# A two-layer diffusion transformer on one core: the FFN's down projection by seven products of quarters, with its sums in seven PSUM banks and the sums of quarters on GpSimd

## The chip, the core and the metric

The kernel runs on one core of a Trainium2 chip. A time is the device time of one execution in microseconds (us). TensorE (PE) does the matrix products, ScalarE (ACT) and VectorE (DVE) the elementwise work, GpSimd (POOL) some more of it, and SyncE (SP) issues most DMAs.

## The reference, cut to what matters

Two layers work on 256 context and 1024 latent tokens of width 1024. Each has a mixing part (windowed attention and a Fourier mix), which the change leaves alone, and then the feed-forward network:

```python
def swiglu(h, w_gate, w_up, w_down):
    return (jax.nn.silu(h @ w_gate) * (h @ w_up)) @ w_down
...
        hf = modulate(rmsnorm(x_mid, norm_pre_ffn[i]), sh2, sc2)
        x = x_mid + g2 * rmsnorm(swiglu(hf, w_gate[i], w_up[i], w_down[i]), norm_post_ffn[i])
```

The hidden width is 2816. The context tokens go through the same weights; in the second layer only the latent tokens go through the FFN.

## The kernel before

Features lie on partitions, tokens along the free dimension. The FFN works on two blocks of tokens: two of 640 in layer 0, two of 512 in layer 1. The hidden width is 22 tiles of 128, taken as `NP` = 11 pairs f. A product in f32 is made of three in f16: an operand is split into hi (a rounded copy, made on ACT) and lo (the rest, made on DVE by a SCALAR_TENSOR_TENSOR from the source and hi), and PE adds hi by hi, lo by hi and hi by lo in PSUM.

**Up and gate** (`ffn_up`) multiply two by two quarters by seven products instead of eight: a pair of weight tiles and a half of the width against two halves of a block. `sums` makes the weight's quarters and their four sums (L499 to L502, 128x512 each, on DVE) and the hi and lo parts (L487 and L488); it does so for the first `AHEAD` = 4 pairs in an earlier stage (tiles `wa`, kept in DRAM as `wc`), and in the last part of up and gate for the other seven (tiles `ww`, 14 of gate and up per layer). `product` inside `ffn_up` (PE, L1116) leaves sums in PSUM, from which DVE and ACT assemble a 2 by 2 of quarters C11 to C22; hi and lo of these (L1163, L1164) are the hidden operand. Eight of the first block's eleven pairs are kept in SBUF (`KEPT`), the others go to DRAM (`hs`) and are read again.

**Down** (`ffn_down`) takes one block in a pass: for each output tile m of eight and each group of `PAIRS` it loads the weights (512 or 384 KB), makes hi (L1253, ACT) and lo (L1254, DVE) pair by pair in 128x256, and PE (L1261) runs through both halves of the pair over the whole block. Two PSUM tiles take turns, and ACT moves a finished one out (L1267). Layer 0 has two passes. Layer 1 has three: its second block is done in two halves, so that the norm of the first half runs beside the products of the second.

`postnorm` is the norm after the FFN: `stats` and `spread` (PE transposes into a PSUM tile, ACT copies), `scale` (L741, DVE) and the addition of the residual read from DRAM (L813, on DVE, or every second one on POOL with `share`). `mod(i)` makes a third of the next layer's modulation vectors on DVE (L674).

Parts are written as Python generators that `mix` interleaves by given costs; the scheduler of the framework then fixes the order of each engine, and pools (four `raw` tiles, eight `w`, five `tmp`, two double PSUM tiles `sc` and four single ones `ps`) bound how far a part runs ahead.

## Time and profile before

| | |
|---|---|
| median of three runs | 2480.28 us (2477.31 to 2480.35) |
| profiled execution, its time | 2482.05 us |
| its span, mean granted PE clock | 2480.2 us, 0.984 |
| up and gate, layer 0 | 564.4 to 1106.6 us |
| down, layer 0 | 1108.6 to 1411 us |
| up and gate, layer 1 | 1806.5 to about 2229 us |
| down, layer 1 | 2231 to 2463 us |
| from the last product to the end | 17.2 us |

Busy times are sums over the instructions of an engine, and a stage is a stretch between the first and the last product of its line. In a row of groups stand line, engine, operation, what is written and read, shapes and count, then busy time and mean ns, then the idle time of the engine just before them with what ended it. In a row of a timeline stand start and length in us.

### The profile page before, as it was taken

The page shows a single profiled execution, that of the slowest core. Times are in us where ns is not written, and L with a number is a line of the kernel's source. Part 1 is how long each engine was busy: PE and PEld are TensorE (multiplying, and loading weights), DVE is VectorE, ACT ScalarE, POOL GpSimd, SP SyncE. Part 2 cuts the span into 40 slices and gives each one's busy share as a digit, 9 for nine tenths or more (in the row PEclk, how much of TensorE's full clock was granted, in tenths as well). Part 3 has the DMA queues.
Part 4 walks back from the last instruction along what each step waited for, and adds up shares of the span by engine and source line. Part 5 has one row for each costly group of instructions (what it writes and reads, how often), then busy time and mean ns, then how long its engine had stood idle before and what let it go on. Part 6 is the DMA issues. An engine that isn't in the chain of part 4 may idle for free. (4 is left out here: it accounts for less than half of the span.)

```text
span 2480.2 us, 44040 instructions
## 1 busy us (share of the span) xinstructions
PE 2353.2 (95%) x17212; PEld 1867.4 (75%) x17212; DVE 1695.2 (68%) x3434; ACT 1347.7 (54%) x2587; POOL 190.5 (8%) x200
## 2 busy tenths in 40 slices
...
GB/s 308 177 134 188 129 146 132 146 260 254 198 187 145 113 130 162 145 183 361 285 254 154 87 127 50 35 18 52 203 340 208 159 60 86 77 117 240 132 251 128
DMA packets 157377, 406.83 MB, mean 164 GB/s; under 512 B 17488, under 2 KB 34288, under 8 KB 157168
## 3 DMA queue, kind: packets, MB, share of 16 engines
...
q14 instruction: 74, 0.61, 0.1%
...
## 5 line engine op out<-in xcount | busy, mean ns | idle before, releaser
L1116 PE MATMUL p<-ffn,ww 128*128 128x320 f16 (+1 forms) x7392 | 926.8, 288 | 34.2 <-ACT ww L487 7.8
L1116 PEld LDWEIGHTS <-ww 128*128 128x128 f16 x7392 | 724.0, 98 | 233.3 <-issue 27.7
L1261 PEld LDWEIGHTS <-wd 128*128 128x128 f16 x3696 | 362.2, 98 | 166.3 <-ACT wd L1253 9.1
L1261 PE MATMUL acc<-hid,wd 128*128 128x320 f16 (+2 forms) x2544 | 334.4, 293 | 6.1 <-ACT wd L1253 5.8
L1254 DVE SCALAR_TENSOR_TENSOR wd<-raw,dn,wd 128x256 f16<-128x256 f32 x440 | 187.4, 480 | 132.8 <-ACT wd L1253 126.7
L543 PE MATMUL accn<-arena,hi 128*128 128x320 f32 (+1 forms) x992 | 260.9, 332 | 1.7 <-DVE PTX L234 0.7
L1253 ACT ACTIVATE wd<-raw,dn 128x256 f16<-128x256 f32 x440 | 187.2, 496 | 130.7 <-PE acc L1261 81.5
L543 PE MATMUL acc<-arena,hi 128*128 128x320 f32 (+2 forms) x928 | 209.5, 331 | 4.9 <-ACT X L1070 3.1
L1261 PE MATMUL acc<-X,wd 128*128 128x320 f16 (+1 forms) x1152 | 191.9, 328 | 2.7 <-ACT wd L1253 2.4
L543 PEld LDWEIGHTS accn<-arena,hi 128*128 128x128 f32 x992 | 174.1, 190 | 18.4 <-issue 7.5
L543 PEld LDWEIGHTS acc<-arena,hi 128*128 128x128 f32 x928 | 155.1, 191 | 23.6 <-issue 6.6
L543 PE MATMUL accn<-arena,lo 128*128 128x320 f32 (+1 forms) x496 | 159.3, 324 | 0.0
L703 POOL TENSOR_TENSOR nr<-nm,mhalf 128x5 f32<-128x5 f32 (+2 forms) x17 | 18.8, 1105 | 1699.3 <-DVE nm L702 1699.3
L216 DVE TENSOR_REDUCE ng<-score 128x1 f32<-128x641 f32 (+2 forms) x144 | 107.1, 745 | 57.8 <-PE score L209 56.1
L487 ACT ACTIVATE ww<-raw,sp 128x1024 f16<-128x1024 f32 x112 | 110.0, 1033 | 67.2 <-DVE raw L502 50.5
L416 DVE TENSOR_TENSOR lo<-raw,hi 128x1024 fp32r<-128x1024 f32 x77 | 99.2, 1289 | 66.6 <-ACT hi L415 50.0
L488 DVE SCALAR_TENSOR_TENSOR ww<-raw,sp,ww 128x1024 f16<-128x1024 f32 x112 | 125.8, 1146 | 25.0 <-ACT ww L487 24.9
L543 PE MATMUL acc<-arena,lo 128*128 128x320 f32 (+2 forms) x464 | 125.7, 328 | 0.0
L217 ACT ACTIVATE A<-score,ng 128x641 f32<-128x641 f32 (+2 forms) x144 | 106.6, 741 | 34.9 <-DVE ng L216 19.5
L415 ACT CAST hi<-raw 128x1024 fp32r<-128x1024 f32 x77 | 80.6, 1047 | 75.4 <-PE acc L543 33.0
L464 ACT ACTIVATE junk<-raw 128x1024 bf16<-128x1024 f32 x88 | 92.4, 1052 | 40.5 <-DMA raw<-in_wup 21.1
L690 DVE TENSOR_TENSOR ssq<-ssq,sq 128x640 f32<-128x640 f32 (+2 forms) x119 | 89.8, 755 | 31.5 <-ACT sq L689 28.6
...
## 6 DMA issues: line engine op xcount, KB each, us to landing
...
```

Of the source, the lines that this page charges most:

```text
L216: nc.vector.tensor_reduce(self.ng[:, hs], sv, axis=AX.X, op=ALU.max, negate=True)
L217: nc.scalar.activation(p, sv, AF.Exp, bias=self.ng[:, hs], accum_out=self.su[:, hs])
L416: nc.vector.tensor_tensor(lo[:, 0:w], raw[:, 0:w], hi[:, 0:w].bitcast(F32), op=ALU.subtract)
L464: self.nc.scalar.activation(junk[:], raw[j][:], AF.Square, accum_out=self.ss[:, j, i:i + 1])
L487: nc.scalar.activation(hi, src, AF.Copy, scale=s)
L488: nc.vector.scalar_tensor_tensor(lo, src, s, hi, op0=ALU.mult, op1=ALU.subtract)
L543: self.nc.tensor.matmul(ps, wt[:, ks], xt[:, a:b], start=(k == 0 and i == 0), stop=(k == n - 1 and i == 2))
L690: nc.vector.tensor_tensor(s[:, 0:w], s[:, 0:w], t[:, 0:w], op=ALU.add)
L1116: nc.tensor.matmul(ps, w[:, at:at + P], G[k // 2][:, k % 2, x, c, 0:h], start=(start and k + t == 0), stop=(k == KD // 2 - 1 and t == 2), ...
L1253: nc.scalar.activation(wt[:, 0, c], raw[:, c], AF.Copy, scale=r)
L1254: nc.vector.scalar_tensor_tensor(wt[:, 1, c], raw[:, c], r, wt[:, 0, c], op0=ALU.mult, op1=ALU.subtract)
L1261: nc.tensor.matmul(out, wt[:, e, k], xs[x][:, s, u:v], start=(f + s + i == 0), stop=(f == NP - 1 and s == 1 and i == 2))
```

## The change

The down projection becomes seven products of quarters too, once for each of four output tiles m (with m + 4) and each pair f, over half a block each: 4 x 11 x 7 x 3 products for a block. Their sums over all eleven pairs stay in seven PSUM banks (three single tiles and the two double ones), so the evacuation, one ACT copy and seven SCALAR_TENSOR_TENSOR of DVE from PSUM (L1325), comes once for each m, in the course of its last three pairs. The norm's `spread` uses single PSUM tiles for that reason.

A weight step loads 256 KB of four quarters, and three instructions of POOL make the sums (L1282, L1284, L1285: 128x256 and twice 128x128); ACT and DVE then make hi and lo of seven quarters at once (128x896, L1289). `LOOK` = 3 steps are made ahead, and the first ones begin before the last products of up and gate.

The hidden operand has seven quarters as well: four sums on POOL for each block and pair (L1174 to L1177), hi and lo in four pieces, and four DMAs to and from DRAM in the place of two. Four of eleven pairs of the first block are kept in SBUF; the second block's are read while the first's last row of products frees their places.

In `sums`, the four additions of a fresh weight go to POOL; those made ahead stay on DVE. `mod(2)` moves from the first down pass into up and gate. The norm of a block in layer 0 and the operands of the next layer work in the place of the result (`Y`). In layer 1 the second block is one pass, and the norms of its two halves follow it, both with `share`.

On DVE, in layer 0's first down pass, before (`wd` are down's weights, `wa` the next layer's up weights made ahead, the ISA rows the modulation):

```order
L1254 SCALAR_TENSOR_TENSOR wd<-raw,dn_120,wd 128x256
L674 ISA wm,half<-wm,c,bada 128x512
L674 ISA half 128x1
L1254 SCALAR_TENSOR_TENSOR wd<-raw,dn_120,wd 128x256 x3
L674 ISA wm,half<-wm,c,bada 128x512
L674 ISA half 128x1
L488 SCALAR_TENSOR_TENSOR wa<-raw,sp_114,wa 128x1024
```

The same engine and place after (L493 is the old L488, `dacc` the seven banks):

```order
L1289 SCALAR_TENSOR_TENSOR wd<-raw,dn_120,wd 128x896 x2
L493 SCALAR_TENSOR_TENSOR wa<-raw,sp_114,wa 128x1024
L1289 SCALAR_TENSOR_TENSOR wd<-raw,dn_120,wd 128x896 x4
L1325 SCALAR_TENSOR_TENSOR A<-dacc,dback_122,A 128x320 x2
L1325 SCALAR_TENSOR_TENSOR A<-dacc,dneg_124,A 128x320
L1289 SCALAR_TENSOR_TENSOR wd<-raw,dn_120,wd 128x896
```

The modulation has left this place, the lo parts are fewer and longer, and evacuations stand between them.

On POOL, in the last part of layer 0's up and gate, after (`raw` the fresh weight's quarters, `hsum` the hidden sums). Before, the first four of these lines stood on DVE as L499 to L502, and POOL had nothing there:

```order
L505 TENSOR_TENSOR raw<-raw 128x512
L506 TENSOR_TENSOR raw<-raw 128x512
L1174 TENSOR_TENSOR hsum<-A 128x320
L1175 TENSOR_TENSOR hsum<-A 128x320
L507 TENSOR_TENSOR raw<-raw 128x512
L1176 TENSOR_TENSOR hsum<-A,hsum 128x320
L508 TENSOR_TENSOR raw<-raw 128x512
L1177 TENSOR_TENSOR hsum<-hsum,A 128x320
```

Weight sums and hidden sums now share one queue, in which one stands behind the other.

On DVE, the end of the program before (L690 adds squares for the norm, L741 scales, L813 adds the residual):

```order
L1254 SCALAR_TENSOR_TENSOR wd<-raw,dn_121,wd 128x256 x3
L690 TENSOR_TENSOR ssq<-ssq,sq 128x256 x6
...
L741 SCALAR_TENSOR_TENSOR X<-X,scl_108,r 128x256 x8
L813 TENSOR_TENSOR X<-res,X 128x256 x4
```

and after (the same lines are L696, L750 and L821):

```order
L1325 SCALAR_TENSOR_TENSOR X<-dacc,dneg_125,X 128x256
L696 TENSOR_TENSOR ssq<-ssq,sq 128x256 x7
...
L750 SCALAR_TENSOR_TENSOR X<-X,scl_108,r 128x256 x10
L821 TENSOR_TENSOR X<-res,X 128x256
L750 SCALAR_TENSOR_TENSOR X<-X,scl_108,r 128x256 x6
L821 TENSOR_TENSOR X<-res,X 128x256 x7
```

Sixteen scalings stand behind the last product where eight stood.

The diff, cut to its core:

```diff
-PAIRS = [(0, 4), (4, 8), (8, 11)]
+DUOS = [(f, min(f + 2, NP)) for f in range(0, NP, 2)]
-KEPT = 8
+KEPT = (0, 1, 4, 5)
+ORDERS = [(0, 1, 4, 5, 2, 3, 6, 7, 8, 9, 10), tuple(range(NP))]
+LOOK = 3
+SEVEN = [(1, 3, 0), (5, 2, 0), (2, 0, 0), (4, 1, 1), (3, 1, 0), (6, 0, 1), (0, 2, 1)]
...
-        self.hs = tc.dram_tile([2, NP, 2, P, 2 * BW], F16, name="hs")
+        self.hs = tc.dram_tile([2, NP, P, 14 * HB], F16, name="hs")
...
     def sums(self, l, i, raw, out, keep):
...
-        nc.vector.tensor_tensor(a22, a21, a22, op=ALU.add)
-        nc.vector.tensor_tensor(a21, a11, a21, op=ALU.subtract)
-        nc.vector.tensor_tensor(a11, a22, a11, op=ALU.subtract)
-        nc.vector.tensor_tensor(a12, a12, a11, op=ALU.subtract)
+        eng = nc.vector if keep else nc.gpsimd
+        eng.tensor_tensor(a22, a21, a22, op=ALU.add)
+        eng.tensor_tensor(a21, a11, a21, op=ALU.subtract)
+        eng.tensor_tensor(a11, a22, a11, op=ALU.subtract)
+        eng.tensor_tensor(a12, a12, a11, op=ALU.subtract)
...
     def spread(self, key, w):
...
-        ps = self.sc.tile([P, 1024], F32, tag="sc", name="rps")
-        for t in range(w // P):
-            nc.tensor.transpose(ps[:, P * t:P * t + P], r[:, t:t + 1].broadcast_to([P, P]), self.ident)
         rr = self.rp.tile([P, BW], F32, tag="r", name="r")
-        nc.scalar.copy(rr[:, 0:w], ps[:, 0:w])
+        for a in range(0, w, 384):
+            b = min(w, a + 384)
+            ps = self.ps.tile([P, 512], F32, tag="ps", name="rps")
+            for t in range(a // P, b // P):
+                nc.tensor.transpose(ps[:, P * t - a:P * t + P - a], r[:, t:t + 1].broadcast_to([P, P]), self.ident)
+            nc.scalar.copy(rr[:, a:b], ps[:, 0:b - a])
...
     def ffn_up(self, l, blocks, seq, hooks):
...
+            t13, t24 = (self.tmp.tile([P, 2, HB], F32, tag="t", name="hsum") for _ in range(2))
+            T1, T3, T2, T4 = (t[:, i, 0:h] for t in (t13, t24) for i in range(2))
+            nc.gpsimd.tensor_tensor(T1, C11, C12, op=ALU.subtract)
+            nc.gpsimd.tensor_tensor(T3, C22, C12, op=ALU.add)
+            nc.gpsimd.tensor_tensor(T2, C22, T1, op=ALU.subtract)
+            nc.gpsimd.tensor_tensor(T4, T2, C21, op=ALU.subtract)
...
-            kept = blk == 0 and f < KEPT
-            if kept:
-                hi, lo = self.keep(f, blocks)
-            else:
-                hi, lo = (self.tmp.tile([P, 4 * HB], F16, tag="t", name="hid")[:, 0:4 * h] for _ in range(2))
-            hv, lv = (v.rearrange("p (q n) -> p q n", q=4) for v in (hi, lo))
-            nc.scalar.activation(hv, src, AF.Copy, scale=s)
-            nc.vector.scalar_tensor_tensor(lv, src, s, hv, op0=ALU.mult, op1=ALU.subtract)
-            if not kept:
-                for part, v in enumerate((hi, lo)):
-                    nc.sync.dma_start(self.hs[blk, f, part, :, 0:4 * h], v)
+            kept = self.keep(f, blocks) if blk == 0 and f in KEPT else None
+            for j, v in ((0, to[:, 0:2, 0:h]), (3, to[:, 2:3, 0:h]), (1, t13[:, :, 0:h]), (2, t24[:, :, 0:h])):
+                if kept:
+                    hi, lo = (kept[j][:, e] for e in range(2))
+                else:
+                    n = (2 if j == 3 else 4) * h
+                    t = self.tmp.tile([P, 4 * HB], F16, tag="t", name="hid")[:, 0:n]
+                    hi, lo = (t.rearrange("p (e n c) -> p e n c", e=2, c=h)[:, e] for e in range(2))
+                nc.scalar.activation(hi, v, AF.Copy, scale=s)
+                nc.vector.scalar_tensor_tensor(lo, v, s, hi, op0=ALU.mult, op1=ALU.subtract)
+                if not kept:
+                    nc.sync.dma_start(self.hs[blk, f, :, 4 * h * j:4 * h * j + n], t)
...
+    def fetch(self, blk, f):
+        at = 0
+        for v in self.places[blk][f]:
+            n = 2 * v.shape[2] * v.shape[3]
+            self.nc.sync.dma_start(v.rearrange("p e n c -> p (e n c)"), self.hs[blk, f, :, at:at + n])
+            at += n
...
+    def down_weights(self, l, blk, m, f, raw):
+        nc = self.nc
+        q = lambda i, j: raw[:, P * i:P * j]
+        r = self.dn[blk][:, f:f + 1]
+        nc.gpsimd.tensor_tensor(q(4, 6).rearrange("p (i c) -> p i c", i=2), q(1, 3).rearrange("p (i c) -> p i c", i=2),
+                                q(0, 1).unsqueeze(1).broadcast_to([P, 2, P]), op=ALU.subtract)
+        nc.gpsimd.tensor_tensor(q(6, 7), q(4, 5), q(2, 3), op=ALU.add)
+        nc.gpsimd.tensor_tensor(q(7, 8), q(3, 4), q(6, 7), op=ALU.subtract)
+        t = self.w.tile([P, 2, 1024], F16, tag="w", name="wd")
+        hi, lo = (t[:, e, 0:7 * P] for e in range(2))
+        nc.scalar.activation(hi, q(1, 8), AF.Copy, scale=r)
+        nc.vector.scalar_tensor_tensor(lo, q(1, 8), r, hi, op0=ALU.mult, op1=ALU.subtract)
+        return t
+    def ffn_down(self, l, blk, w, dst, free=None):
+        nc, h = self.nc, w // 2
+        back, neg = self.dback[blk][:, 1].bitcast(F32), self.dneg[blk][:]
+        todo = [(m, f) for m in range(KD // 2) for f in ORDERS[blk]]
+        raws, made = [], []
+        def load():
...
+        def make():
...
+        for _ in range(LOOK):
+            load()
+        yield 0
+        for _ in range(LOOK):
+            make()
+        yield 0
+        if self.acc is None:
+            self.acc = [self.ps.tile([P, 512], F32, tag="ps", name="dacc") for _ in range(3)]
+            two = [self.sc.tile([P, 1024], F32, tag="sc", name="dacc") for _ in range(2)]
+            self.acc += [t[:, 512 * i:512 * i + 512] for t in two for i in range(2)]
+        acc = [a[:, 0:h] for a in self.acc]
+        stt = lambda out, i, by, add: nc.vector.scalar_tensor_tensor(out, acc[i], by, add, op0=ALU.mult, op1=ALU.add)
+        for m in range(KD // 2):
+            C11, C12, C21, C22 = (dst(m + 4 * i)[:, h * j:h * j + h] for i in range(2) for j in range(2))
+            order = ORDERS[blk]
+            for group in [order[i:i + 1] for i in range(NP - 3)] + [order[NP - 3:]]:
+                while (raws or todo) and len(made) < len(group) + LOOK:
+                    make()
+                now = [(f, made.pop(0)) for f in group]
+                for i, (a, j, c) in enumerate(SEVEN):
+                    for f, wt in now:
+                        for n, (e, x) in enumerate(((0, 0), (1, 0), (0, 1))):
+                            nc.tensor.matmul(acc[i], wt[:, e, P * a:P * a + P], self.places[blk][f][j][:, x, c],
+                                             start=(f == order[0] and n == 0), stop=(f == order[-1] and n == 2))
+                            t += h / 2400
+                    if len(group) > 1:
+                        with self.tc.high_priority(offset=100):
+                            if i == 0:
+                                nc.scalar.activation(C11, acc[0], AF.Copy, scale=back)
+                            elif i == 1:
+                                stt(C12, 1, back, C11)
+                            elif i == 2:
+                                stt(C11, 2, back, C11)
+                            elif i == 3:
+                                stt(C21, 3, neg, C12)
+                            elif i == 4:
+                                stt(C22, 4, back, C21)
+                                stt(C12, 4, back, C12)
+                            elif i == 5:
+                                stt(C12, 5, back, C12)
+                            else:
+                                stt(C21, 6, neg, C21)
+                if free and m == KD // 2 - 1:
+                    for f in group:
+                        free(f)
...
     def program(self):
...
+            follow = {1: (2, 3), 3: (4, 5), 7: (6, 7), 10: (8, 9, 10)}
+            def free(f):
+                for g in follow.get(f, ()):
+                    self.fetch(1, g)
+            down = [self.ffn_down(l, 0, w, first, free),
+                    self.ffn_down(l, 1, w, lambda m: self.X[:, m, a1:b1])]
+            def early():
+                next(down[0])
+                self.hidden(l, blocks)
+                for f in (2, 3, 6, 7):
+                    self.fetch(0, f)
+            up = self.ffn_up(l, blocks, seq, {((1, NP - 1, 0), 5): early, ((1, NP - 1, 1), 1): lambda: self.down_scale(0),
+                                              ((1, NP - 1, 1), 5): lambda: next(down[0])})
             mix((part(up, 14 * AHEAD - 2), 2 * AHEAD * one), (side, 46))
             mix((part(up, 14 * AHEAD - 7), 2 * AHEAD * one), (self.down_norms(l), 24))
-            mix((up, one * (44 - 4 * AHEAD)), (mod(0, 1), 64), (iter(()) if last else self.norms(l + 1), 2 * AHEAD))
-            places, rest = self.hidden(l, blocks)
-            down = lambda blk, c0, c1, dst: (self.ffn_down(l, blk, places, c0, c1, dst), cost(KD, KH_, c1 - c0))
-            first = lambda m: self.Y[:, m, 0:w]
-            (a0, b0), (a1, b1) = blocks
+            mix((up, one * (44 - 4 * AHEAD)), (mod(0, 1, 2), 96), (iter(()) if last else self.norms(l + 1), 2 * AHEAD))
+            self.hidden_far(l, w // 2)
+            for f in (8, 9, 10):
+                self.fetch(0, f)
+            def rest():
+                for f in range(2):
+                    self.fetch(1, f)
+                    yield
             norm = self.postnorm(l, 1, a0, b0, done, y=first)
+            c = 42 * NP * w / 2400
             if not last:
-                pre, side = self.ahead(l + 1), mod(2)
-                mix(down(0, 0, w, first), (part(pre, 4 * AHEAD), 4 * AHEAD), (side, 32), (rest, 14))
+                pre = self.ahead(l + 1)
+                mix((down[0], c), (part(pre, 4 * AHEAD), 4 * AHEAD), (rest(), 4))
                 self.down_scale(1)
-                side = chain(norm, self.xstats(*A, "A"), self.scaled(l + 1, 0, *A, "A"))
-                mix(down(1, 0, w, lambda m: self.X[:, m, a1:b1]), (side, 32), (pre, 8 * AHEAD))
+                side = chain(norm, self.stats(first, w, "A"), self.scaled(l + 1, *A, "A", first))
+                mix((down[1], c), (side, 32), (pre, 4 * AHEAD))
                 self.new_arena((l + 1) % 2)
-                run(self.operands(l + 1, *A))
+                run(self.operands(l + 1, *A, first))
                 first, side = self.postnorm(l, 1, a1, b1, done), self.xstats(*B, "B")
             else:
-                mix(down(0, 0, w, first), (rest, 14))
+                mix((down[0], c), (rest(), 4))
                 self.down_scale(1)
-                h = w // 2
-                m = a1 + h
-                mix(down(1, 0, h, lambda k: self.X[:, k, a1:m]), (norm, 13))
-                mix(down(1, h, w, lambda k: self.X[:, k, m:b1]), (self.postnorm(l, 1, a1, m, done), 14))
-                run(self.postnorm(l, 1, m, b1, done, share=True))
+                mix((down[1], c), (norm, 16))
+                m = a1 + w // 2
+                mix((self.postnorm(l, 1, a1, m, done, share=True), 14), (self.postnorm(l, 1, m, b1, done, share=True), 14))
```

143 lines of the change are left out of this document (66 added, 77 removed).

## The prediction

> **What bounds the kernel now.** I read the page's first part, then the windows of the stages that the change touches, then groups by line with shapes kept apart, last the timelines.
>
> ```profile
> PE 2353.2 (95%) x17212; PEld 1867.4 (75%) x17212; DVE 1695.2 (68%) x3434; ACT 1347.7 (54%) x2587; POOL 190.5 (8%) x200
> ...
> core 0: us, PE busy (x) PEld busy (x) DVE busy (x) ACT busy (x) POOL busy (x), PEclk, DMA share, GB/s
> 758.00:1106.60 348.60, 330.33 (x2389) 233.26 (x2387) 269.29 (x554) 166.28 (x261) 0.00 (x0) 0.99 0.44 140
> 1106.60:1411.00 304.40, 295.94 (x2157) 212.11 (x2156) 204.85 (x421) 146.19 (x270) 2.33 (x2) 0.98 0.68 239
> 1965.00:2231.00 266.00, 261.32 (x2396) 233.08 (x2394) 193.07 (x367) 140.20 (x234) 0.00 (x0) 1.00 0.26 84
> 2231.00:2463.00 232.00, 231.46 (x1605) 156.76 (x1603) 140.69 (x340) 131.51 (x311) 1.71 (x2) 1.00 0.61 196
> 2463.00:2480.20 17.20, 1.27 (x6) 0.81 (x6) 7.32 (x18) 1.11 (x3) 3.81 (x5) 0.58 0.29 92
> ```
>
> The rows are the last part of up and gate in layer 0, its down projection, the same two of layer 1, and the tail. TensorE is busy throughout at a granted clock near 1, and POOL does nothing in the two ups. The clock of 0.98 to 1.00 leaves nothing to win there. So in both down projections PE is the bound, VectorE has 100 and 91 us to spare, and in layer 0's up VectorE has 79.
>
> ```profile
> 1109.22 12.94 PE L1261 MATMUL acc<-X,wd 128*128 128x320 f16 x94 [0.18 <-DVE wd L1254]
> 2439.83 22.98 PE L1261 MATMUL acc<-hid,wd 128*128 128x256 f16 x209
> 1127.97 6.63 PE L1261 MATMUL acc<-hid,wd 128*128 128x320 f16 x36 [5.80 <-ACT wd L1253]
> ```
>
> Here PE runs without a gap: 12.94/94 = 0.138 us for a product of 320 columns, 22.98/209 = 0.110 for 256. The third row is the one stall of layer 0's down.
>
> **What PE gives back.** Per layer and block the old form has 8 x 11 x 2 x 3 = 528 products of the block's width, which is 1056 of half its width, so 2112 for two blocks; the new one 4 x 11 x 7 x 3 = 924, so 1848. Alone, the new products take 1848 x 0.138 = 255 us in layer 0 and 1848 x 0.110 = 203 in layer 1, against the stages' 304 and 232.
>
> **What it asks of POOL and VectorE.** Each of the 176 weight steps (44 for each of four passes) puts three sums on POOL, 128x256 and twice 128x128, and one lo part of 128x896 on VectorE in the place of five or six of 128x256. Prices:
>
> ```profile
> L885 POOL TENSOR_TENSOR kr<-kr,sw 128x320 f32<-128x320 f32 x4 | 3.4, 869 | 0.2
> L884 POOL TENSOR_TENSOR sw<-sw,A 128x64 f32<-128x64 f32 x1 | 0.3, 323 | 0.0
> ...
> L488 DVE SCALAR_TENSOR_TENSOR ww<-raw,sp,ww 128x1024 f16<-128x1024 f32 x84 | 106.2, 1280 | 25.0 <-ACT ww L487 24.9
> L488 DVE SCALAR_TENSOR_TENSOR ww<-raw,sp,ww 128x512 f16<-128x512 f32 x28 | 20.9, 745 | 0.0
> L1147 DVE SCALAR_TENSOR_TENSOR A<-p,inv,A 128x320 f32<-128x320 f32 x22 | 12.0, 545 | 6.9 <-PE p L1116 6.8
> ```
>
> POOL: (869 - 323)/256 = 2.13 ns a column and 187 ns beside, so 0.73 + 0.46 + 0.46 = 1.65 us a step, 1.28 for 512 columns. The lo part, between VectorE's rows, 1.045 ns a column: 1.15 us at 896. Two of 1024 in a row take 2.46 below, 1.23 each and not 1.28, so I take 1.10.
>
> What these cost each other is the open question, and before shows it in two places.
>
> ```profile
> 212.68 2.46 DVE L488 SCALAR_TENSOR_TENSOR wa<-raw,sp,wa 128x1024 f16<-128x1024 f32 x2
> 212.69 3.19 POOL L885 TENSOR_TENSOR X<-X,sw 128x320 f32<-128x320 f32 x1
> ...
> 517.59 11.46 DVE L741 SCALAR_TENSOR_TENSOR X<-X,scl,r 128x256 f32<-128x256 f32 x16
> 518.68 1.76 POOL L813 TENSOR_TENSOR X<-res,X 128x640 f32<-128x640 f32 x1 [6.82 <-DVE X L741]
> 521.91 1.69 POOL L813 TENSOR_TENSOR X<-res,X 128x640 f32<-128x640 f32 x1 [1.47 <-DVE X L741]
> 525.08 1.70 POOL L813 TENSOR_TENSOR X<-res,X 128x640 f32<-128x640 f32 x1 [1.48 <-issue]
> ...
> L741 DVE SCALAR_TENSOR_TENSOR X<-X,scl,r 128x256 f32<-128x256 f32 x8 | 3.8, 477 | 2.7 <-ACT r L720 2.7
> ...
> 211.73 0.88 POOL L884 TENSOR_TENSOR sw<-sw,A 128x320 f32<-128x320 f32 x1 [5.43 <-DVE sw L882]
> 211.95 0.80 DVE L216 TENSOR_REDUCE ng<-score 128x1 f32<-128x641 f32 x1
> ...
> L216 DVE TENSOR_REDUCE ng<-score 128x1 f32<-128x641 f32 x96 | 78.5, 817 | 30.9 <-PE score L209 30.0
> ```
>
> In the first pair POOL's sum, 0.87 by itself, takes 3.19: it is done 0.7 us after two instructions of VectorE that lost nothing. In the second, sixteen scalings take 11.46 where 16 x 0.477 is 7.63: VectorE lost 3.8 us of the 5.15 that POOL ran, a share of 0.74. In the third, VectorE reads PSUM and neither is slower. So instructions of VectorE with two operands in SBUF and those of POOL take turns, and both sums and lo parts are of that kind. The Trainium skill ("SBUF — State Buffer", section "SBUF: two separate sides") has a sharper rule: whichever starts first keeps the shared ports for its whole instruction and the other fully blocks. By it VectorE would lose all 5.15 and not 3.8, and layer 0's down below would have 378 for its upper end in the place of 340; the measured share stands in my sum.
>
> **Layer 0's down.**
>
> ```profile
> L1254 DVE SCALAR_TENSOR_TENSOR wd<-raw,dn,wd 128x256 f16<-128x256 f32 x176 | 75.7, 479 | 57.5 <-ACT wd L1253 51.5 <-DMA hid<-hs 5.9
> L674 DVE CUSTOM_DVE_ANT_0 wm<-wm,c,bada 128x512 f32<-128x512 f32 x16 | 11.7, 744 | 0.0
> L674 DVE CUSTOM_DVE_ANT_0 wm<-wm,c,half 128x512 f32<-128x512 f32 x16 | 11.6, 746 | 0.2
> ...
> L1254 DVE SCALAR_TENSOR_TENSOR wd<-raw,dn,wd 128x256 f16<-128x256 f32 x263 | 111.3, 481 | 75.2 <-ACT wd L1253 75.1
> ```
>
> VectorE's 204.9, less 75.7 of lo parts and 23.3 of the modulation that moves out, leaves 105.9. It gets 88 lo parts (96.8) and 2 x 4 x 7 = 56 evacuations that read PSUM (0.545 each, 30.5): 233. POOL's 88 x 1.65 = 145 would cost VectorE 0.74 of it, 107: 340 if every sum falls on such work. If all turns fall into gaps, PE's 255 is left and some 11 us at the starts of the two passes (the stall above, 5.8, and another like it): 266. Neither end is nearer to a row; I take the middle, 303, against the stage's 304: **-1, -38 to +36**.
>
> **Layer 1's down.** Other work 140.7 - 111.3 = 29.4, of which some 8 moves into the tail; 96.8 of lo parts and 56 evacuations at about 0.48 (26.9): 145. With 107 for POOL it would be 252; with none PE's 203 and 6 for the starts, 209. Within a step POOL's sums (1.65) and VectorE's lo part (1.10) exclude each other: 88 x 2.75 = 242 if they follow each other strictly. PE's own step is 2.31, so this pair is the longer one. The 3.19 us row is the nearest, for there POOL waited out each of VectorE's instructions; I take 242: **+10, -23 to +20**.
>
> **Up and gate.**
>
> ```profile
> L502 DVE TENSOR_TENSOR raw<-raw 128x512 f32<-128x512 f32 x14 | 9.6, 689 | 0.2
> L674 DVE CUSTOM_DVE_ANT_0 wm<-wm,c,half 128x512 f32<-128x512 f32 x32 | 23.6, 748 | 6.1 <-DMA wm<-in_wada 5.1 <-DMA c<-cs 0.8
> L1164 DVE SCALAR_TENSOR_TENSOR hid<-A,hp,hid 128x1280 f16<-128x1280 f32 x10 | 15.5, 1550 | 3.7 <-ACT hid L1163 3.5
> L1164 DVE SCALAR_TENSOR_TENSOR X<-A,hp,X 128x1280 f16<-128x1280 f32 x4 | 6.2, 1546 | 2.4 <-ACT X L1163 2.4
> ```
>
> In layer 0's last part VectorE gives up four sums for 14 weights (4 x 9.6 = 38.4), gets 32 modulation instructions (23.6), and its 14 hidden lo parts become three of 640 and one of 320 (3.18 in the place of 1.55, +22.9): 269.3 + 8.1 = 277.4. POOL gets 56 hidden sums of 320 (48.7) and 56 weight sums of 512 (71.7), 120 us, of which 0.74 is 89: 366 at most against a stage of 349, and 277 at least, where PE keeps the bound and nothing changes. Besides, a fresh weight's chain grows from 4 x 0.69 to 4 x 1.28 us, behind up to 3.5 us of hidden sums in POOL's queue, and
>
> ```profile
> L1116 PE MATMUL p<-ffn,ww 128*128 128x320 f16 (+1 forms) x7392 | 926.8, 288 | 34.2 <-ACT ww L487 7.8
> ```
>
> PE already waits on that chain. 0.3 to 2.5 us more for 14 weights and the turns: I take **+10, 0 to +35**. Layer 1: VectorE 193.1 - 38.4 + 20 (1.44 more for each of 14 hidden sets) = 175, POOL (56 x 0.73 + 71.7) x 0.74 = 83, together 258 under the stage's 266: only the chain, **+5, 0 to +20**. The earlier up parts have no fresh sums on POOL and VectorE has room there; zero.
>
> **Tail.**
>
> ```profile
> 2467.90 4.66 DVE L741 SCALAR_TENSOR_TENSOR X<-X,scl,r 128x256 f32<-128x256 f32 x8 [1.25 <-ACT r L720]
> 2476.99 0.42 DVE L813 TENSOR_TENSOR X<-res,X 128x256 f32<-128x256 f32 x1 [3.44 <-DMA res<-xs]
> ```
>
> Layer 1's last block is now one pass, so the norm of its first half no longer runs beside the second: eight more scalings (4.7), four more sums on VectorE (1.7) and part of a second statistics chain, with residual reads that already come last: **+8, 4 to 14**.
>
> **At nothing.** SP's more and smaller reads (176 of 256 KB for weights, four pieces per hidden set) hide behind a DMA share of 0.6 to 0.7, with three weights read ahead. If that cover goes at a pass's start, the second block's hidden sets that follow the first's (eight of 1.15 MB, at 239 GB/s some 38 us, spread over a last row of products of 32 us) would stall PE by 5 to 20 us. The block's norm in its own place and the changed banks move no work onto PE's path.
>
> **The sum.** -1 + 10 + 10 + 5 + 8 = +32 on the profiled execution's 2482.05: 2514. That run lies 1.8 above the median of 2480.28, so 2512.
>
> **Rivals.** (1) The turns fall into gaps and PE stays the bound: layer 0's down 266 (-38), layer 1's 209 (-23), up 0, tail +8: -53, 2427 by the median; with up's +15 it is 2442. For it: VectorE's work alone stays under PE's in both downs and three steps are made ahead. Against it: the sixteen scalings lost 0.74 of POOL's time. It decides where POOL's step with its waits stays under PE's 2.89 us (21 products) in layer 0 and 2.31 in layer 1. (2) POOL starves: where VectorE issues without a gap, POOL waits out two of its instructions as in the 3.19 row. If a step takes 1.65 + 2 x 1.10 = 3.85 us in half of the steps, layer 0's down comes to its upper end of 340 and layer 1's to 44 x (2.75 + 3.85) = 290, and with +35 and +20 in the ups it is 36 + 58 + 55 + 8 = +157; half of that, which I find likelier since a lo part of down itself waits for POOL, gives 2559. (3) Gains and losses cancel within 0.2%, 2475 to 2485, about what a measurement of this kernel can tell from no change.
>
> **Chances.** The forecast (turns pace the downs, 2485 to 2545) 0.48; rival 1 0.28; rival 2 0.18; rival 3 0.06. So faster 0.28, same 0.06, slower 0.66. The range: rival 1's lower half is left out (2425), and above, the worst of rival 2 beyond 2590.
>
> **What would show it.** In the profile after: downs near 303 and 242 us with PE busy 255 and 203 and idle time that ends on ACT or VectorE weights made from POOL's sums; POOL's three sums per step at well over 1.65 us; lo parts over 1.10. Rival 1 shows PE without gaps; rival 2 POOL means over 1 us for 128 columns, and PE stalls on fresh weights in up. The prediction is wrong if POOL's price for 128 columns is not the line through 64 and 320, or if the lost share of 0.74 is no rule where VectorE has gaps.

## The result

The changed kernel takes 2694.7 us (median of four runs, 2686.42 to 2696.66) against 2480.32 before (four runs), a ratio of 1.0858 with a 95% interval of 1.0832 to 1.0884: 214 us slower, outside the range given. The forecast was slower by 32 us. The profiled execution, the fastest of the four, spans 2684.6 us, 204.4 more than before; the tables below go by it.

A stage's time below runs from the start of its line's first product to the end of its last, read from the two traces:

| us | before | after | difference | forecast |
|---|---|---|---|---|
| up and gate, layer 0 | 543.8 | 589.6 | +45.8 | +10 (0 to 35) |
| down, layer 0 | 302.3 | 388.1 | +85.8 | -1 (-38 to 36) |
| between | 395.7 | 393.3 | -2.4 | 0 |
| up and gate, layer 1 | 424.7 | 454.8 | +30.1 | +5 (0 to 20) |
| down, layer 1 | 231.8 | 266.4 | +34.6 | +10 (-23 to 20) |
| from the last product to the end | 17.4 | 28.7 | +11.3 | +8 (4 to 14) |

Four of the five terms lie outside their own ranges, all on the slow side. The page of after, the same parts as before:

```profile
PE 2368.2 (88%) x17212; PEld 1889.2 (70%) x17212; DVE 1859.5 (69%) x3302; ACT 1383.7 (52%) x2446; POOL 920.4 (34%) x1020
...
L1289 DVE SCALAR_TENSOR_TENSOR wd<-raw,dn,wd 128x896 f16<-128x896 f32 x176 | 215.1, 1243 | 162.2 <-ACT wd L1288 161.2
L1288 ACT ACTIVATE wd<-raw,dn 128x896 f16<-128x896 f32 x176 | 178.5, 1038 | 285.5 <-POOL raw L1285 254.9
...
L1282 POOL TENSOR_TENSOR raw<-raw 128x256 f32<-128x256 f32 x176 | 163.9, 933 | 221.7 <-DMA raw<-in_wdown 208.1
```

and from the groups of the whole span the other two sums:

```profile
L1284 POOL TENSOR_TENSOR raw<-raw 128x128 f32<-128x128 f32 x176 | 120.5, 688 | 7.5
L1285 POOL TENSOR_TENSOR raw<-raw 128x128 f32<-128x128 f32 x176 | 117.2, 669 | 7.4
```

POOL went from 190 to 920 us. The last columns give the chain of a weight step: VectorE waits for ACT, ACT for POOL's last sum (L1285), and POOL for the read of the weights. The chain so ends at a read of 256 KB, which the forecast had priced at nothing. The windows, on the stages of the first table:

```profile
core 0: us, PE busy (x) PEld busy (x) DVE busy (x) ACT busy (x) POOL busy (x), PEclk, DMA share, GB/s
758.00:1153.50 395.50, 352.78 (x2467) 243.99 (x2466) 324.79 (x629) 196.38 (x319) 154.34 (x125) 0.96 0.50 166
1153.50:1350.00 196.50, 144.59 (x927) 92.92 (x924) 120.57 (x143) 74.44 (x81) 101.81 (x130) 0.89 0.69 235
1350.00:1541.60 191.60, 151.30 (x977) 101.48 (x978) 140.51 (x180) 78.83 (x98) 95.83 (x129) 0.89 0.47 151
2122.00:2389.50 267.50, 247.14 (x2206) 215.71 (x2204) 184.51 (x329) 146.41 (x256) 121.39 (x113) 0.99 0.28 92
2389.50:2521.00 131.50, 108.17 (x925) 91.83 (x924) 75.60 (x93) 51.83 (x57) 98.61 (x133) 0.92 0.60 193
2521.00:2656.00 135.00, 111.98 (x940) 94.33 (x938) 86.10 (x107) 50.07 (x64) 94.70 (x124) 0.94 0.41 129
```

In layer 0's down no engine is full: PE idles 92 us of 388 (52 and 40 in the two passes), VectorE is at 67%, POOL at 51%. That looks like a loop that waits for its own latency. In layer 1's down POOL is at 73%. PE's busy time in layer 0's down is 295.9 us, that of before, with 264 products fewer, which should have given back 36 us. Its granted clock fell from 0.98 to 0.89, and products at half the clock, counted further down, make some 23 of the 36.

The waits, whose columns are total us, times and longest, first in the first pass of layer 0, then of layer 1:

```profile
POOL raw L1282 <- DMA raw<-in_wdown: 83.8, 27, 16.7
ACT wd L1288 <- POOL raw L1285: 75.8, 30, 4.8
...
ACT wd L1288 <- POOL raw L1285: 57.0, 22, 9.6
...
POOL raw L1282 <- DMA raw<-in_wdown: 25.1, 9, 10.2
```

POOL waits 84 us for reads in the one and 25 in the other. Beside the width of a block, the passes differ by the next layer's weights made ahead (`wa`), which layer 0 makes beside its down and layer 1 does not. In e13 below, without them, POOL's wait for reads in layer 0's first pass is 43 us.

A steady stretch in layer 1, POOL's timeline over four steps of weights:

```profile
2431.09 0.72 POOL L1282 TENSOR_TENSOR raw<-raw 128x256 f32<-128x256 f32 x1
2431.89 1.18 POOL L1284 TENSOR_TENSOR raw<-raw 128x128 f32<-128x128 f32 x1
2433.04 1.57 POOL L1282 TENSOR_TENSOR raw<-raw 128x256 f32<-128x256 f32 x1
2434.57 0.45 POOL L1285 TENSOR_TENSOR raw<-raw 128x128 f32<-128x128 f32 x1
...
2440.77 0.72 POOL L1282 TENSOR_TENSOR raw<-raw 128x256 f32<-128x256 f32 x1
```

VectorE's timeline, where the lo parts of the first two of these steps end:

```profile
2436.13 2.74 DVE L1289 SCALAR_TENSOR_TENSOR wd<-raw,dn,wd 128x896 f16<-128x896 f32 x2 [0.73 <-ACT wd L1288]
```

and SP's, which issues reads into the tiles that come free:

```profile
2437.63 1.59 SPq L1306 DMA_DIRECT2D raw<-in_wdown  x2
```

The same 128x128 sum takes 0.45 or 1.18 us, and the 128x256 one 0.72 or 1.57: the short ones are POOL's own price (0.46 and 0.73 were forecast), the long ones contain a turn of VectorE. SP issues the next read when the first of VectorE's two lo parts is through (2437.63) and POOL begins with it at 2440.77, four steps after 2431.09: 9.68 us, or 2.42 a step, against PE's 2.31. The window of these 9.68 us, with the columns of the windows above:

```profile
2431.09:2440.77 9.68, 9.68 (x83) 8.37 (x82) 8.01 (x10) 4.04 (x6) 9.37 (x13) 0.92 0.40 107
```

POOL is busy for 9.37 us of it, and SP refills a raw tile as soon as it is free, but PE too runs without a gap, 83 products at a granted clock of 0.92. So this stretch shows three limits close together, and not which of them sets the pace.

### The profile page after: what moved, and what is told of

The parts are those of the page before. It is cut to its first block, busy times and chain, and to the rows that moved or that the text cites. A ratio compares the mean times of both kernels' runs of the same rounds, so it can differ in the third digit from the quotient of the medians.

```text
span 2684.6 us, 45745 instructions
## 1 busy us (share of the span) xinstructions
PE 2368.2 (88%) x17212; PEld 1889.2 (70%) x17212; DVE 1859.5 (69%) x3302; ACT 1383.7 (52%) x2446; POOL 920.4 (34%) x1020
## 4 chain that ended last, share of the span: by engine, by line
PE 25%; DVE 12%; DMA 10%; POOL 7%; issue 6%; ACT 5%; SPq 0%; POOLq 0%; DVEq 0%; ACTq 0%
PE p L1138 11%; DMA raw<-in_wdown 4%; PE dacc L1337 4%; PE accn L549 4%; POOL raw L1282 2%; DVE wd L1289 2%; DMA wm<-in_wada 2%; POOL raw L1284 2%; POOL raw L1285 2%; PE acc L549 1%; DVE hid L1196 1%; ACT wd L1288 1%; PE pv L258 1%; DMA hs<-hid 1%; DMA hid<-hs 1%
## 5 line engine op out<-in xcount | busy, mean ns | idle before, releaser
L1138 PE MATMUL p<-ffn,ww 128*128 128x320 f16 (+1 forms) x7392 | 951.5, 291 | 80.7 <-DVE A L1157 11.7
L1337 PEld LDWEIGHTS <-wd 128*128 128x128 f16 x3696 | 371.5, 102 | 268.8 <-ACT wd L1288 73.7
L1337 PE MATMUL dacc<-hid,wd 128*128 128x320 f16 (+1 forms) x2688 | 379.8, 300 | 113.5 <-ACT wd L1288 50.6
L1289 DVE SCALAR_TENSOR_TENSOR wd<-raw,dn,wd 128x896 f16<-128x896 f32 x176 | 215.1, 1243 | 162.2 <-ACT wd L1288 161.2
L1288 ACT ACTIVATE wd<-raw,dn 128x896 f16<-128x896 f32 x176 | 178.5, 1038 | 285.5 <-POOL raw L1285 254.9
L1282 POOL TENSOR_TENSOR raw<-raw 128x256 f32<-128x256 f32 x176 | 163.9, 933 | 221.7 <-DMA raw<-in_wdown 208.1
L908 POOL TENSOR_TENSOR qs<-X,qs 64x256 fp32r<-64x256 f32 x72 | 58.3, 810 | 328.3 <-ACT qs L907 323.0
L1337 PE MATMUL dacc<-X,wd 128*128 128x320 f16 (+1 forms) x1008 | 144.0, 297 | 20.7 <-ACT A L1343 7.8
L1174 POOL TENSOR_TENSOR hsum<-A 128x320 f32<-128x320 f32 (+1 forms) x44 | 43.1, 980 | 336.4 <-DVE A L1161 216.4
L493 DVE SCALAR_TENSOR_TENSOR ww<-raw,sp,ww 128x1024 f16<-128x1024 f32 x112 | 128.6, 1166 | 26.0 <-ACT ww L492 25.8
L505 POOL TENSOR_TENSOR raw<-raw 128x512 f32<-128x512 f32 x28 | 41.9, 1497 | 279.9 <-DVE ww L493 271.0
```

The source lines that it names most:

```text
L493: nc.vector.scalar_tensor_tensor(lo, src, s, hi, op0=ALU.mult, op1=ALU.subtract)
L908: nc.gpsimd.tensor_tensor(qs[b, o::2, :], src, qs[a, o::2, :].bitcast(F32), op=ALU.subtract)
L1138: nc.tensor.matmul(ps, w[:, at:at + P], G[k // 2][:, k % 2, x, c, 0:h], start=(start and k + t == 0), stop=(k == KD // 2 - 1 and t == 2), ...
L1282: nc.gpsimd.tensor_tensor(q(4, 6).rearrange("p (i c) -> p i c", i=2), q(1, 3).rearrange("p (i c) -> p i c", i=2), q(0, 1).unsqueeze(1).bro ...
L1288: nc.scalar.activation(hi, q(1, 8), AF.Copy, scale=r)
L1289: nc.vector.scalar_tensor_tensor(lo, q(1, 8), r, hi, op0=ALU.mult, op1=ALU.subtract)
```

## The experiments

Every kernel is the changed one with the edit shown; each ran once with a profile, beside one run of the kernel before (2473.8 to 2477.9 us). The stage times are read as above:

| run | time | up 0 | down 0 | up 1 | down 1 |
|---|---|---|---|---|---|
| before (profiled) | 2482.05 | 543.8 | 302.3 | 424.7 | 231.8 |
| after (profiled) | 2686.42 | 589.6 | 388.1 | 454.8 | 266.4 |
| e1 six raw, six w tiles | 2645.68 | 599.0 | 363.2 | 447.2 | 257.7 |
| e2 down's sums on VectorE | 2671.49 | 590.3 | 381.1 | 453.9 | 253.0 |
| e3 up's weight sums on VectorE | 2699.47 | 592.4 | 394.3 | 450.0 | 265.6 |
| e4 no sums in down | 2601.04 | 589.2 | 340.5 | 454.8 | 225.3 |
| e5 no hidden sums | 2663.88 | 577.5 | 390.3 | 445.7 | 262.1 |
| e6 modulation back in down | 2704.89 | 578.7 | 412.9 | 454.4 | 268.3 |
| e7 eight tmp, six w tiles | 2734.77 | 585.7 | 415.4 | 466.4 | 277.6 |
| e8 weight reads from ACT | 2681.45 | 590.0 | 394.2 | 454.4 | 256.9 |
| e9 late hidden reads | 2714.58 | 588.7 | 396.5 | 470.0 | 265.8 |
| e10 e1 and e4 | 2563.00 | 596.9 | 326.7 | 439.5 | 223.2 |
| e11 up's additions undone | 2658.81 | 563.7 | 410.6 | 429.9 | 266.8 |
| e12 e1, e2 and e9 | 2627.45 | 600.5 | 362.5 | 446.9 | 242.5 |
| e13 nothing made ahead in down | 2640.13 | 588.7 | 317.1 | 455.0 | 263.7 |
| e14 e12, e13 and e6 | 2597.08 | 587.3 | 304.0 | 449.2 | 245.4 |
| e15 e11 and e3 | 2636.70 | 552.0 | 405.7 | 431.0 | 260.4 |
| e16 e13 and e4 | 2589.63 | 589.5 | 282.2 | 465.3 | 226.6 |
| e17 e13 and e9 | 2642.39 | 592.4 | 312.2 | 454.3 | 260.6 |

Stages that an edit does not touch differ between runs: up in layer 0 by 4 us, the downs by 6 and 8, and up in layer 1 by 1, but for two runs that are 15 and 10 over (470 in e9 and 465 in e16). The likely reason, not shown, is that the scheduler orders the whole program anew. Four runs of the changed kernel itself lie within 10 us. A single run's difference of such a size is not read as an effect.

**The sums of down: e1, e2, e4.** The first question was whether a step waits for POOL's turns or for a free raw tile.

```diff
-  tc.tile_pool(name="raw", bufs=4) ... tc.tile_pool(name="w", bufs=8)
+  tc.tile_pool(name="raw", bufs=6) ... tc.tile_pool(name="w", bufs=6)      # e1
-        nc.gpsimd.tensor_tensor(q(4, 6) ...   (and the two others)
+        nc.vector.tensor_tensor(q(4, 6) ...                                # e2
-        nc.scalar.activation(hi, q(1, 8), AF.Copy, scale=r)                # e4, with the three sums
+        src = q(1, 2).unsqueeze(1).broadcast_to([P, 7, P])
+        nc.scalar.activation(hi, src, AF.Copy, scale=r)
```

> Six raw tiles in the place of four, paid for by six w tiles in the place of eight; nothing else. Theory R (the ring): a weight step of down holds its raw tile from the read's issue over POOL's sums, ACT and VectorE to the release, 9.7 us in layer 1, so four tiles give a step every 2.4 us at best and more with any delay; with six tiles the ring alone would allow 1.6, so layer 1's down falls from 266 us to 220-240 and layer 0's from 388 to 310-340. Theory T (turns): POOL's three sums, 2.3 us a step with the waits for VectorE, pace the step; both downs stay within 10 us of 266 and 388. Theory Q (queues): stalls at the starts of passes and behind the norm's scalings make the loss; they stay, and only some 10 to 20 us go. Up may lose some us by the fewer w tiles in every theory.

> The three sums of a weight step of down are on VectorE in the place of POOL. Theory T: VectorE gets 0.99 us a step (0.42 + 2 x 0.29), loses no turns, and the sums no longer wait: layer 1's down 245 us (29 other + 88 x 2.14 + 27), layer 0's 325. Theory R: the ring's cycle falls from 9.7 to some 7 us by the shorter sums, so layer 1's falls too, to 240-250, while layer 0's stays above 350 because the weights made ahead still hold raw tiles two by two. Theory Q: VectorE's queue gets longer, so the stalls behind it grow; no gain, 266 or more in layer 1.

> Down's three sums a step are left out: hi and lo are made of one loaded quarter read seven times, so ACT, VectorE, PE and the reads are as before and the result is another. Theories T and R both: layer 1's down falls to 215-225 us; layer 0's under T to 290-310 (VectorE 106 + 97 + 31, PE 255, starts), under R to 310-340, because the ring is still shared with the weights made ahead. Theory Q: 250 or more in layer 1, 350 or more in layer 0.

e1 gave 363 and 258. In layer 0 the gain of 25 us lies between the theories; in layer 1 the 9 us lie within T's 10, and 7 of them are the gap at the start, which fell from 12.0 to 5.3 us. e7 below has six w tiles with four raw ones (and eight tmp tiles) and stands at 415 and 278. If the tmp tiles change nothing in down, the two more raw tiles are worth 52 and 20 us at equal w tiles, and the smaller w ring cost a part of what the larger raw ring brought. e2 gave 253 in layer 1, 8 over T's 245, and 381 in layer 0, where R had said over 350 and T 325: T falls there. e4 gives the price of the sums: 41 us in layer 1, which comes to 225 as T and R said, and 48 in layer 0, which stays at 340, the upper end of R. Without any sum layer 0's down is still 38 us slower than before.

**The weights made ahead: e10, e13, e16.**

```diff
-            early = chain(self.norms(l), self.ahead(l)) if l == 0 else iter(())
+            early = chain(self.norms(l), self.ahead(l)) if l == 0 else self.ahead(l)   # e13
...
-                mix((down[0], c), (part(pre, 4 * AHEAD), 4 * AHEAD), (rest(), 4))
+                mix((down[0], c), (rest(), 4))
```

> Six raw tiles and six w tiles, and down's sums left out as before (one quarter read seven times, so the result is another). With the ring and the sums both gone only the starts and the queues are left: theories R, T and D together say 210-218 us in layer 1 (203 of products and the start) and 295-315 in layer 0. If the w tiles are now what ends the waits, both stay at the values of the run with no sums and four raw tiles, 340 and 225, or above.

> The next layer's weights made ahead move from layer 0's two down passes to layer 1's attention, where layer 0 has its own. Theory W (they hold raw tiles two by two and stand in ACT's queue behind issues that wait for hidden stores): layer 0's gap of 17.4 us falls under 8, and the weight steps come as in layer 1 (266/88 = 3.0 us a step there, where PE's step is 2.3): layer 0's down falls from 388 us to 305-330. Rival (VectorE's load: the weights made ahead were 41 us of it, and its turns): 345-360 with the gap still over 12. Layer 1's attention grows by 0 to 30 us, up in layer 1 stays.

> The weights made ahead moved to layer 1's attention, and down's sums left out (one quarter read seven times, so the result is another). With the sums the first alone gave 317 us in layer 0, and the sums alone left out gave 340. If the two causes are separate, 317 - 25 to 317 - 41 = 276-292 us in layer 0, of which 255 are products; if the weights made ahead were slow only because of POOL's sums, 300 or more.

e10 missed: 327 and 223, only 14 and 2 under e4, so six raw tiles, paid for by two w tiles, did not take away what the sums had left in layer 0. e13 found a larger part: 317 us, 71 less, within the range of W (305 to 330) and far from the rival's 345 to 360. Part of that comes back: layer 1's attention takes 31 us more (424 between the stages in the place of 393), and the time is 46 under the profiled run of after. Only its expectation for the gap failed (14.2 us and not under 8; see below). e16 takes both away: 282 us, in the range for separate causes. So in layer 0's down the weights made ahead are worth 58 to 71 us, the sums 35 to 48, both together 106 of the 133 us by which the stage exceeds its products (1848 x 0.138 = 255). How much of the first is raw tiles held, and how much w tiles, time on ACT and VectorE, or traffic, was not separated. From a read's issue to the end of the last lo part made of it, the weight steps of this stage hold raw tiles for 889 us in sum and the weights made ahead for 494, together 1383 of the 4 x 388 us that four tiles have. So the ring is nearly full, a third of it with the weights made ahead. That alone does not prove that it sets the pace, since in e13 the steps alone take 1095 of 4 x 317.

**The start of a pass: e8, e9, e17.** At the start of layer 0's down PE stands for 17.4 us and then runs on half its clock:

```profile
1182.86 1.51 PE L1337 MATMUL dacc<-hid,wd 128*128 128x320 f16 x5 [17.41 <-ACT wd L1288]
```

The DMA part of the page, for 1153 to 1183 us alone:

```profile
DMA packets 5777, 11.83 MB, mean 394 GB/s; under 512 B 642, under 2 KB 1800, under 8 KB 5774
...
hid<-hs SPq DMA_DIRECT2D x16, 320.0 KB, 6.0
hs<-hid SPq DMA_DIRECT2D x6, 320.0 KB, 5.6
```

It is 11.8 MB in 30 us, 394 GB/s, most of it hidden operands, read (`hid<-hs`) and stored (`hs<-hid`) 320 or 160 KB at a time: some 8.5 of the 11.1 MB issued in these 30 us. The lo part of the fourth weight step, and SP's issue of a read of weights after it:

```profile
1157.92 1.15 DVE L1289 SCALAR_TENSOR_TENSOR wd<-raw,dn,wd 128x896 f16<-128x896 f32 x1
1172.99 0.33 SPq L1306 DMA_DIRECT2D raw<-in_wdown  x1
```

At 1159.07 the first four steps are through and their raw tiles free, but the read of the fifth is issued 14 us later. Hidden reads and stores stand ahead of it in SP's queue, and two reads for the weights made ahead. So this read waits for its place in the queue, and not for a tile.

```diff
-                nc.sync.dma_start(raw[:, 0:512], self.io["wdown"] ...
+                nc.scalar.dma_start(raw[:, 0:512], self.io["wdown"] ...               # e8
-            for f in (8, 9, 10):
-                self.fetch(0, f)
...
-                for f in range(2):
-                    self.fetch(1, f)
+                for blk, f in ((0, 8), (0, 9), (0, 10), (1, 0), (1, 1)):              # e9, with (rest(), 30)
+                    self.fetch(blk, f)
```

> The reads of down's weights are issued from ACT's queue in the place of SP's. Theory Q (the reads stand behind hidden stores and reads in SP's queue that wait for other work): PE's gap of 17.4 us in the first pass of layer 0 and that of 12.0 in layer 1 fall under 7, some of the later waits go as well; layer 0's down comes to 345-370, layer 1's to 248-258. Theory R: only the gaps at the starts go, 370-378 and 255-260, since the ring of four tiles stays. If ACT's queue is delayed by the reads that wait for a free tile, both get worse, 390 and 270 or more.

> Of the hidden reads, those of the first block's last three pairs and of the second block's first two are issued one by one in the course of the first pass, not all at its start. Theory D (at the start of down the DMA engines are full: 11.8 MB in 30 us at 394 GB/s, and the fifth weight step's read comes behind 10 MB of hidden reads and stores): the gap of 17.4 us in layer 0 falls to 4-9 and that of 12.0 in layer 1 to 3-7, and the half clock behind it goes too; down 360-372 and 253-260 us. Theory R alone (the tiles are held by the weights made ahead): the gap of layer 0 stays over 14, that of layer 1 falls since nothing is made ahead there. Up stays within 5 us of 590 and 455.

> The weights made ahead moved to layer 1's attention, and the late hidden reads, nothing else. In the run without weights made ahead SP issues 15 hidden reads in 11.3 us ahead of the next weights' reads, with the DMA engines full. If layer 0's gap at the start has two causes in a row (those reads, and the weights made ahead), each of which was shown alone to leave 14 to 17 us, both together bring it from 14.2 us to under 7, and layer 0's down from 317 to 300-312. If something else makes the gap, 12 us or more stay.

e8 left the gap of layer 0 (17.2 us) and its down (394); layer 1's gap fell to 3.5 us and its down to 257, as Q and R both said. e9 left layer 0's gap too (17.2), while layer 1's fell from 12.0 to 4.5, though not its whole down; the run is slower than the changed kernel (2714.58), and its up in layer 1 takes 470 us, 15 over the 455 expected. The timelines of e9 and of e13 show why late reads alone, and the removal of the weights made ahead alone, leave layer 0's gap. ACT in e9:

```profile
1179.55 0.72 ACT L492 ACTIVATE wa<-raw,sp 128x512 f16<-128x512 f32 x1 [11.86 <-DMA hs<-hid]
```

SP in e13:

```profile
1154.01 11.34 SPq L1253 DMA_DIRECT2D hid<-hs  x15
1165.52 1.18 SPq L1306 DMA_DIRECT2D raw<-in_wdown  x2
```

what SP waited for in e13 in those 11.4 us (total us, times, longest):

```profile
SPq L1253 <- DMA hid<-hs: 3.8, 8, 0.7
```

and PE in e17:

```profile
1173.75 5.61 PE L1337 MATMUL dacc<-hid,wd 128*128 128x320 f16 x26 [5.28 <-ACT wd L1288]
```

In e9 POOL's sums of the fifth step were ready at 1172.9, but ACT's queue stood 11.9 us at the issue of a store of weights made ahead (L496), by the profile until a hidden store had landed. In e13, without that, SP issued fifteen hidden reads ahead of the fifth step's weights, one every 0.75 us. An issue takes 0.32 us there; the rest is waiting, since in this trace SP's DMAs take turns on eight semaphores, and a read is issued only when the one eight before it has landed, after 6.1 us. With both taken away (e17) the gap is 5.3 us, as expected, and down 312, just over the range and 5 us under e13.

**Up and gate: e3, e5, e6, e7, e11, e15.**

```diff
-        eng = nc.vector if keep else nc.gpsimd
+        eng = nc.vector                                                        # e3
-            nc.gpsimd.tensor_tensor(T1, C11, C12, op=ALU.subtract)   (and T3, T2, T4)
-            for j, v in (... (1, t13[:, :, 0:h]), (2, t24[:, :, 0:h])):
+            for j, v in (... (1, to[:, 1:3, 0:h]), (2, to[:, 2:4, 0:h])):      # e5
-            mix((up, ...), (mod(0, 1, 2), 96), ...)
+            mix((up, ...), (mod(0, 1), 64), ...)                               # e6, mod(2) beside down[0]
-  tc.tile_pool(name="tmp", bufs=5) ... "w", bufs=8
+  tc.tile_pool(name="tmp", bufs=8) ... "w", bufs=6                             # e7
+                nc.scalar.activation(hv, src, AF.Copy, scale=s)                # e11: e5, e6, and one
+                nc.vector.scalar_tensor_tensor(lv, src, s, hv, ...)            #   hi and lo of 4 quarters
```

> In up and gate the four sums of a fresh weight are on VectorE again; the hidden sums stay on POOL. Theory T with the longer chain: the 46 us that up lost in layer 0 and the 30 in layer 1 go for the larger part, to 550-560 us and 430-437. Rival: the hidden sums and the four-piece hidden operands are the cost; up stays at 580 or more and 445 or more. The downs keep 388 and 266 within 10 us.

> In up and gate the four hidden sums on POOL are left out, with their two buffers; hi and lo of all four pieces are made from the quarters that are there, so ACT, VectorE's count and the stores are as before and the result is another. Theory V (VectorE is full in up: 325 of 396 us in the last part, stretched by POOL's turns): VectorE's instructions get shorter, up falls from 590 us to 565-578 in layer 0 and from 455 to 435-445 in layer 1. Theory M (the ring of five tmp tiles: six are asked for by a hidden set, more by the modulation's reads): about the same, since two of six are gone. Theory H (the four pieces, their stores and their longer lo parts on VectorE): no change within 6 us.

> The last third of the next layer's modulation goes back from up to the first down pass of layer 0, where it was before; nothing changes in layer 1. Theory V: 32 instructions of 0.75 to 0.9 us leave VectorE's queue in the up of layer 0, which falls from 590 us to 562-575; the down of layer 0, where VectorE waits a third of the time, grows by 0 to 15 from 388. Theory H or M with hidden sets alone: up stays at 580 or more. Either way the total is within 20 us of 2690.

> Eight tmp tiles in the place of five, paid for by six w tiles in the place of eight (the run with six raw tiles had six w tiles as well, and 599 and 447 us in up). Theory M: up falls to 550-570 us in layer 0 and 425-440 in layer 1. Theory V: 590-600 and 445-455. The downs are as with four raw tiles, 388 and 266, within 12 us.

> In up and gate all additions but one are undone: no hidden sums, the modulation's last third back in down, and the hidden operands of pairs that go to DRAM made by one instruction of ACT and one of VectorE as before (their stores keep four pieces and all bytes, the result is another); only the weight sums stay on POOL. Theory V: VectorE's surplus is gone, so up comes to 545-560 us in layer 0 and 426-436 in layer 1 (before 544 and 425). Rival: the stores and the tmp tiles that they hold are the rest; 570 or more and 440 or more. Down in layer 0 is as with the modulation there, 400-420.

> As the run with all of up's additions but the weight sums on POOL undone, and those on VectorE too: what is left in up is only the hidden stores of 14 quarters in the place of 8 and the four pairs kept instead of eight. If the chain through POOL made the rest of 20 us in layer 0 and 5 in layer 1, up comes to 544-552 and 424-428. If the stores make it, it stays at 560 or more and 430.

e3 gains nothing: 592 and 450. It takes the longer chain away but gives VectorE its 38 us of sums back, so it does not show what the chain alone costs. e5 takes 12 and 9 us off, at the weak end of V. e6 takes 11 off layer 0 (579), less than V's 15 to 28, and down in layer 0 grows by 25 us where 0 to 15 were expected. e7 misses M's ranges (586 and 466), but beside e1, which has six w tiles too, up in layer 0 is 13 us shorter, so a share of the tmp ring is not excluded. e11 brings 564 and 430: layer 1 as V said, layer 0 four over it. There e15 gives the rest: with the weight sums on VectorE 552 and 431, so on POOL they cost 12 us in layer 0 once VectorE has room, and nothing in layer 1. Some 8 and 6 us over the kernel before are left, whose cause stays open. The groups of the modulation and of the product with the inverse scale, in the last part of layer 0's up, in after:

```profile
L680 DVE CUSTOM_DVE_ANT_0 wm<-wm,c,half 128x512 f32<-128x512 f32 x47 | 43.7, 941 | 6.3 <-DMA wm<-in_wada 6.3
L1161 DVE SCALAR_TENSOR_TENSOR A<-A,inv 128x960 f32<-128x960 f32 x14 | 21.5, 1537 | 0.2
```

and in e15, where POOL does next to nothing in up:

```profile
L680 DVE CUSTOM_DVE_ANT_0 wm<-wm,c,half 128x512 f32<-128x512 f32 x32 | 23.7, 749 | 5.3 <-DMA wm<-in_wada 4.3 <-DMA c<-cs 0.7
L1161 DVE SCALAR_TENSOR_TENSOR A<-A,inv 128x960 f32<-128x960 f32 x15 | 18.2, 1212 | 0.1
```

Each instruction of the one kind is 192 ns longer and of the other 325 with POOL at work: here VectorE pays for a part of POOL's 154 us in its own queue.

**All together: e12 and e14.**

> Six raw and six w tiles, down's sums on VectorE, and the late hidden reads, together; the result is the reference's. If the three gains add (25 + 7 and 20 in layer 0, 9 + 13 and 8 in layer 1), down is 335-350 us and 235-245, the time 2600-2630. If VectorE is then the bound (325 and 245 us of work by the prices before), 335-345 and 245-255. Either way slower than 2480 by 4 to 6%, since up keeps its 75 us.

> The weights made ahead moved to layer 1's attention, six raw and six w tiles, down's sums on VectorE, late hidden reads, and the modulation's last third back in layer 0's first down pass, together; the result is the reference's. Down in layer 0 290-310 us, in layer 1 240-245, up in layer 0 580-590 and in layer 1 445-455: a time of 2540-2580, still slower than 2480, since up's loss and the tail stay. Rival: the attention of layer 1 has no room for the weights made ahead and the sum stays over 2600.

e12 came to 2627, 363 and 243: the gains add in layer 1 and not in layer 0, where 335 to 350 were expected. e14, the best version with the reference's result, takes 2597.08 us, over the 2540 to 2580 expected and under the rival's 2600. Its four stages came as expected; the sum did not, since layer 1's attention, with the weights made ahead in it, takes 425 us between the stages where it took 393. Layer 0's down is 304 there, what it was before the change. It is 4.8% slower than the run of before beside it (2477.9), so no version found beats the kernel before.

## Why the prediction was wrong

**What bounds the kernel.** PE did bound it, and its products did fall: 1848 at 0.138 and 0.110 us a layer. But a gain that PE gives is paid out only if PE never waits, and after a wait it runs slower. The windows of after behind the gap of layer 0:

```profile
1165.00:1183.00 18.00, 0.59 (x6) 0.63 1.04 397
1183.00:1187.00 4.00, 2.12 (x8) 0.50 0.40 147
1187.00:1191.00 4.00, 4.00 (x19) 0.60 0.80 215
1191.00:1195.00 4.00, 4.00 (x32) 1.00 0.36 121
```

The columns are PE's busy time and products, its granted clock, the DMA share and GB/s. At a clock of 0.5 the products come 0.27 us apart; 171 of layer 0's and 96 of layer 1's do so (at 0.21 there), some 23 and 10 us. The forecast took the clock as settled at 0.98 to 1.00. The Trainium skill ("TensorE: Matmul & The Clock Gate", Part 1, on the clock gate) has the rule that bears on it: after an idle window of some 3.4 us the array gets half its clock, until a window of sustained work is over. The rows agree in the half; the slow stretch is some 7 us long here (1182.9 to 1190.2), and PE worked only 2.12 of its first four.

**Layer 0's down: the failed step.** The term was -1 and measured +86. It added up engine times, each instruction at its price and its turns, and took the middle between a full VectorE and a full PE. No engine was full. The step that failed is the one put at nothing: that SP's reads hide "with three weights read ahead". Before, one raw tile carried four pairs, 48 products of half a block and so 6.6 us of PE; now it carries one, 2.9 us, goes through three POOL instructions, ACT and VectorE before it is free, and the weights made ahead take two tiles at a time, a third of the ring in the mean. The runs showed in its place: 58 to 71 us for the weights made ahead beside the steps, and 35 to 48 for POOL's sums in the chain of a step. That held tiles are the larger part of the first is likely by e1 and e7, but not shown.

The second half of that paragraph named the starts: hidden reads of about 9 MB where the second block follows the first, "5 to 20 us" if the cover went. The stalls came elsewhere, at the start of the first pass, where the first block's own hidden reads and stores stand ahead of the weights in SP's queue: 17 and 12 us, and the half clock behind them.

**Layer 1's down.** The forecast took strict turns of POOL's sums (1.65) and VectorE's lo part (1.10), 88 x 2.75 = 242. Measured: 266 with a start of 12.0 us and some 10 us of half clock, 244 without the two. That this comes near 242 is in part luck, for in the stretch shown above a step takes 2.42 us and not 2.75. PE's waits in the whole stage, in the columns of the waits above:

```profile
PE dacc L1337 <- ACT wd L1288: 17.8, 6, 12.0
PE dacc L1337 <- DVE X L1325: 10.4, 5, 6.4
PE dacc L1337 <- ACT X L1343: 7.2, 3, 3.1
PE dacc L1337 <- DVE wd L1289: 4.4, 6, 1.1
PE dacc L1337 <- DVE A L1325: 3.4, 5, 1.4
PE dacc L1337 <- ACT A L1343: 2.9, 3, 1.4
```

Some 22 us are waits for weights, 12 of them the start, and 24 are waits for the evacuation of the seven banks (L1325, L1343), where the down of before had 0.3 in all (in layer 0's down after they are 19). The forecast had priced the evacuation's work on VectorE, but held that "the changed banks move no work onto PE's path". Without the sums (e4) 4 us of these 24 are left, and the stage falls by 41: so it is the sums that PE waits for, in good part by way of evacuations that come late on VectorE and ACT.

**Turns.** The share of 0.74 of POOL's time was too high where VectorE has gaps. In layer 0's up POOL ran 154 us where 120 were forecast, and VectorE was busy 325 where the forecast's work alone was 277: by this estimate a share of 0.31. In the downs POOL pays the larger part instead. Its three sums take 2.29 us a step in the mean, where the short rows above add up to 1.62, which makes 118 us over 176 steps; the lo part takes 1243 ns with the sums and 1150 without them (e4), which makes 16. By the rule of the Trainium skill ("SBUF — State Buffer", section "SBUF: two separate sides"), the one that starts first blocks the other until its instruction ends. The rows of layer 1 agree for POOL: 1.18 is 0.45 and 0.73 of waiting, less than one lo part of 1.15 to 1.5.

**Up and gate.** The forecast put +10 and +5 on the chain of fresh weights. That size may have been right in layer 0: e11 and e15 put the weight sums on POOL at 12 us there, be it by the chain or by turns. What it lacked is VectorE's load as a whole: hidden sums on POOL (12 and 9 us), the modulation (11), and in layer 1 the four-piece hidden operands, which e11 undoes and e5 does not (16 us, an estimate by difference; in layer 0 it comes to 3). The rows for these loads were in the prediction (277 of 349 us of work and 120 us on POOL); it read 277 against 349 as room. PE's waits in that stretch, before and then after, show that the queue hurts before it is full:

```profile
PE p L1116 <- DVE ww L488: 3.4, 4, 1.7
...
PE p L1116 <- DVE A L1135: 1.2, 3, 0.6
...
PE p L1116 <- DVE A L1123: 0.3, 1, 0.3
...
PE p L1138 <- DVE ww L493: 9.6, 9, 1.6
PE p L1138 <- DVE A L1145: 8.5, 5, 3.8
...
PE p L1138 <- DVE A L1157: 4.8, 3, 2.1
```

L1145 and L1157 (before L1123 and L1135) are VectorE's evacuations of PSUM, which the next products wait for and which stand behind whatever is ahead of them in VectorE's queue.

**Tail.** Right: +11.3 within 4 to 14, and for the reason given. Sixteen scalings now stand where eight stood, and the last additions still wait for the residual's reads:

```profile
2662.12 4.99 DVE L750 SCALAR_TENSOR_TENSOR X<-X,scl,r 128x256 f32<-128x256 f32 x10 [0.33 <-ACT r L728]
2667.38 3.39 DVE L750 SCALAR_TENSOR_TENSOR X<-X,scl,r 128x256 f32<-128x256 f32 x6
2681.02 0.42 DVE L821 TENSOR_TENSOR X<-res,X 128x256 f32<-128x256 f32 x1 [1.86 <-DMA res<-xs]
```

**The rivals.** The turns did not hide (rival 1). Rival 2 had POOL starved and ended at 2559 to 2637; the measured time lies over even that, because the rival, too, counted engines and neither tiles nor queues. Its own sign, POOL means over 1 us for 128 columns, did not come (0.67 and 0.69). Of the two things that were to show the prediction wrong, POOL's price held (0.45 for 0.46) and the share of 0.74 did not. The trace of before had already one stall of 5.8 us at that start; the forecast took its size over unchanged, although the hidden reads there grew.
